# A hybrid attention / SSD backbone in fp32: layer 1's short convolution in token order, and a wider margin for the SSD groups

## The chip, the core and the metric

One NeuronCore of one Trainium2 chip runs the whole program in one launch. The metric is the device time of that launch in microseconds (us). The five engines have their own instruction queues: PE (TensorE, matmuls and transposes), DVE (VectorE), ACT (ScalarE), POOL (GpSimd) and SP (SyncE, which here issues most DMAs). In this program each engine works through its instructions in the order in which they were written, so one that waits holds all that stand behind it on the same engine.

## The reference, cut to what matters

Two layers over 256 latent tokens of width 2048, with 256 context tokens beside the first. Layer 0 (even) joins 16 heads of neighbourhood attention with a bidirectional Mamba-2 SSD of 8 groups; layer 1 (odd) is a gated short convolution. Every layer is normed, modulated by a conditioning vector, and added to the stream through a gate. The part that the change rewrites is layer 1:

```python
def short_conv_mixer(h, w_in, conv_w, w_out):
    p = h @ w_in                                   # 2048 -> 4 * 2048
    bg, cg, hv, g = jnp.split(p, 4, axis=-1)
    y = bg * dw_conv(cg * hv, conv_w)              # 3 taps along the tokens, one set per channel
    return (jax.nn.silu(g) * y) @ w_out
```

The other half of the change touches the order in which layer 0's SSD groups are placed. In a group the decay matrix exp(cs_i - cs_j) between tokens is built for four heads, multiplied with C B^T, and applied to x by matmuls.

## The kernel before

**Arithmetic.** All big projections are fp32 by three fp32r matmuls: activations and weights are each split in a high and a low part (`hH`/`hL`, `WH`/`WL`), and high x high, high x low and low x high are summed in PSUM. A weight block of 128 x 1024 values (512 KB) is loaded by SP into one of five `raw` buffers (`issue`, L367), cast by ACT into one of three places `w` (`split`, L403; the cast has line 422), and its low part is made by DVE (`low_part`, L426; line 429). From the output projection on, three more places are cut out of buffers that are free by then (KL, QT with QL, and wH with wL): six in all. `mm` is line 196, `turn` (a transpose by the identity) line 200.

**Order.** The program has no loop on the chip: Python writes out every instruction once, in an order that a planner decides. `Plan` (L38) keeps a modelled time for each engine and for each buffer. The main line of the program writes the matmuls of the projections, chunk by chunk, and after each few of them calls `pump` (L279), which looks at the tasks in three lists, `urgent`, `side` and `back`. A task is a generator that yields what it needs next: an engine, the buffers that must be ready, and a number of PSUM banks (`W_`). `may` (L247) lets it go on if the plan says that this engine would not have to wait. For PE the line is

```python
return rdy + (0 if isurg else 800) <= now + 100
```

that is, work of a `side` task on PE is let out only when its operands have been ready, by the plan, for 0.7 us. Where the main line cannot go on (no free bank, a row not made yet), `force` (L300) takes the task that can start earliest, without asking `may`. Tasks also hold shares of two budgets: 9 buffers `tmp` of 128x512 and 8 `half` of 128x256. `take` gives the buffer that was used longest ago.

**SSD groups.** `group_gen(s, gi)` (L1503) runs for each of 8 groups as a `side` task with 4 `tmp` and 4 `half` (spawned in `do_ssd`, L1640). Its steps: C B^T on PE; two reads for each half of the group of decay rows from DRAM scratch `csr` by SP (L1524); ACT and DVE steps (L1533 to L1553) that end in the product `Ds` of decay and C B^T (L1553, DVE); 16 matmuls `bank<-tmp,xtm` on PE, for which the task waits by `W_("PE", Ds[3], nb=1)`, and after which its `tmp` are given back; then gate, squares, a matmul that sums them (`sqs[0]`), a power on POOL (L1595), a transpose of the factor (`r2`), DVE (L1605), and `put_mix` (L1003, with lines 1008 and 1010), which splits the rows for the output projection. The output projection of layer 0 takes the pairs of mix rows in the order 0 to 5, 8 to 15, 6, 7 (L565); the last SSD group's pair is number 15, so 14th in that order. Its first pass makes two column groups of 512 at once.

**Layer 1.** For each of four column blocks i (512 channels) the parts cg, hv, g, bg are projected in this order, each with 8 weight blocks of 12 matmuls (96), into two PSUM banks (token tiles t = 0, 1; 128 tokens on the partitions). Each part is followed by an `urgent` task, and `ordered` (L1992) lets these tasks run one after the other:

- `cg_gen` (L2012): ACT copies cg out of PSUM.
- `hv_gen` (L2020): DVE makes u = hv x cg (L2025). Then `over` (L2003) turns u, four 128x128 transposes for each pair of channel tiles, so that channels lie on the partitions. Now a tap is a scalar of a partition: ACT multiplies the middle tap (L2032), DVE adds the two shifted taps (L2036, L2038) out of PSUM into v. All taps carry a factor 0.5 (`scwh`, L988).
- `gg_gen` (L2042): sg = (tanh(g/2) + 1) g, in token order (L2045, L2047).
- `bg_gen` (L2050): sg times bg (L2053); `over` turns the product; DVE multiplies it with v (L2058); ACT and DVE split the result into high and low (L2064, L2066) as `y2`, the stationary operand of the last projection.

Then four parts of 96 matmuls with `sc_out` follow, each ended by `fin_gen` (L2094).

Of the kernel before, what the change touches and what calls it, by code (L numbers as in the profile page):

```python
# [8 lines left out]
F32 = mybir.dt.float32  # L9
F32R = mybir.dt.float32r  # L10
AF = mybir.ActivationFunctionType
ALU = mybir.AluOpType
# [25 lines left out]
class Plan:  # L38
# [5 lines left out]
    def __init__(self):  # L44
        self.t = dict.fromkeys(("PE", "DVE", "ACT", "POOL", "SP"), 0.0)
        self.w, self.r, self.last = defaultdict(float), defaultdict(float), defaultdict(float)
        self.dma = 0.0
        self.pool = (0.0, 0.0)
# [85 lines left out]


class Task:
    def __init__(self, gen, tmps=0, halves=0):
        self.gen, self.tmps, self.halves, self.cond, self.on = gen, tmps, halves, None, False


@with_exitstack
def kernel(ctx: ExitStack, tc, x, cx, ada0, w0, adaT, w_in, w_out, sc_in, sc_out, rpb, small, const,
                       strict, rows, out):
    nc = tc.nc
    PS = bass.MemoryType.PSUM
    sb = ctx.enter_context(tc.tile_pool(name="sb", bufs=1))
# [3 lines left out]
    V, S, G, T, DMA = nc.vector, nc.scalar, nc.gpsimd, nc.tensor, nc.sync  # L150
    DMA2 = nc.scalar
    plan = Plan()
    E = plan.add

    def st(shape, tag, dt=F32, name=None):
        return sb.tile(list(shape), dt, tag=tag, name=name or tag, bufs=1)
# [29 lines left out]
    def take(pool):  # L186
        b = min(pool, key=lambda a: plan.last[a.tensor.name])
        pool[:] = [a for a in pool if a is not b]
        return b

    tmp, half, raw_ = (lambda: take(free_t)), (lambda: take(free_h)), (lambda: take(free_r))
# [6 lines left out]
    def turn(o, i):  # L198
        k = i.shape[0]
        E(T.transpose(o, i, ident if k == 128 else ident[:k, :k]))  # L200


    urgent, side, back = [], [], []
# [2 lines left out]
    budget = [NTMP, NHALF]  # L206
    reserve = [0]

    def spawn(q, gen, tmps=0, halves=0):
        q.append(Task(gen, tmps, halves))  # L210

    def cap(task, tmps, halves):
        budget[0] += task.tmps - tmps
# [26 lines left out]
    def grow(task):  # L240
        _, t, h = task.cond
        if t - task.tmps > budget[0] or h - task.halves > budget[1]:
            return False
        cap(task, t, h)
        return True

    def may(task, hor, isurg):  # L247
        eng, aps, nb = task.cond
        if eng == "if":
            return aps()  # L250
        if eng == "grow":
            return grow(task)
        if nb and len(free_b) < nb + (0 if isurg else reserve[0]):
            return False
        if eng == "DVE":
            lows_try()
        now, t = plan.t["PE"], plan.t["ACT" if eng == "AQ" else eng]
        rdy = plan.ready(aps)
        if eng == "AQ":
            return t <= now + hor and rdy <= t  # L260
        if hor < 2000 and nb and sorted(plan.last[b.tensor.name] for b in free_b)[nb - 1] + 3000 > now:
            return False
        if hor < 2000:
            rdy += 4000 if eng == "PE" else 2000 if eng == "DVE" else 0
        if eng == "PE":
            if nb:
                rdy = max(rdy, sorted(plan.last[b.tensor.name] for b in free_b)[nb - 1])
            return rdy + (0 if isurg else 800) <= now + 100
        if eng == "SP":
            return rdy <= max(t, now) + 200  # L270
        return t <= now + hor and rdy <= max(t, now) + 400
# [79 lines left out]
    P_ = lambda n: sm[:, _off[n][0]:_off[n][1]]  # L351
# [311 lines left out]
    hH, hL = [None] * KB, [None] * KB  # L663
# [320 lines left out]
    E(V.tensor_scalar(out=cwh, in0=P_("cw"), scalar1=0.5, scalar2=None, op0=ALU.mult))  # L984
    cbh = st([128, 32], "cbh")
    E(V.tensor_scalar(out=cbh, in0=P_("cb"), scalar1=0.5, scalar2=None, op0=ALU.mult))
    scwh = st([128, 48], "scwh")
    E(V.tensor_scalar(out=scwh, in0=P_("scw"), scalar1=0.5, scalar2=None, op0=ALU.mult))  # L988
    gqk = st([128, 1], "gqk")
    E(V.scalar_tensor_tensor(out=gqk, in0=P_("qg"), scalar=float(128 ** -0.5), in1=P_("kg"), op0=ALU.mult, op1=ALU.mult))  # L990

# [386 lines left out]
    Btm = [None]  # L1378
# [245 lines left out]
    def do_ssd(s, nxt):  # L1624
        if s:
            psB = banks(2)
            proj(256, 512, psB, 1)
            spawn(urgent, make_b(s, psB), 3)
        psC, = banks(1)
        proj(256, 256, [psC], 4)  # L1630
        spawn(urgent, make_c(s, psC), 0, 2)
        psX = banks(4)
        proj(512, 512, psX, 2)
        for gi in range(2):
            spawn(urgent, make_x(s, gi, psX[2 * gi:2 * gi + 2]), 3)
        psZ = banks(2)
        proj(512, 256, psZ, nxt)
        spawn(urgent, silu2_gen("Z", s, psZ, sz, lambda: ssd_done[0] >= 2 * s and ("K", 0) in got), 1)
        for gi in range(2):
            spawn(side, group_gen(s, gi), 4, 4)  # L1640

    spawn(urgent, make_b(0, psB0), 3)
    do_g(0, 1)
# [3 lines left out]
    for k in range(2):  # L1647
        W, _ = use()
# [4 lines left out]
        used()  # L1653
    spawn(urgent, dt_gen(psD), 1, 3)
    do_ssd(0, 2)

    def do_qk(a, nxt):
# [99 lines left out]
    late = [None] * 8 + \  # L1757
# [162 lines left out]
    for ns in ((0, 512), (1024,), (1536,)):  # L1920
        pss = [banks(2) for n in ns]
        for ip in range(16):
# [8 lines left out]
            if hold[0]:  # L1931
# [49 lines left out]


    y2 = [None] * KB
    scw = scwh.rearrange("p (k c) -> p k c", k=3)
    flat = lambda ap: ap.rearrange("p b c -> p (b c)")
    v = st([128, 4, 256], "Btm", name="v")
    cg, u = [], []
    sg = [st([128, 512], f"V{k}", name=f"sg{k}") for k in "HL"]

# [30 lines left out]
    def hv_gen(i, ps):  # L2020
        for t in range(2):
            yield W_("DVE", ps[t])
            if i == 0:
                u.append(tmp())
            E(V.tensor_tensor(out=u[t], in0=ps[t], in1=cg[t], op=ALU.mult))  # L2025
            give(free_b, ps[t])
        for b in range(0, 4, 2):
            pt = yield from over(u, b)
            yield W_("ACT", pt)
            for k in range(2):  # L2030
                ch = 4 * i + b + k
                E(S.mul(v[:, b + k, :], pt[:, k * 256:k * 256 + 256], scw[:, 1, ch:ch + 1]))  # L2032
            for k in range(2):
                ch, o = 4 * i + b + k, k * 256
                yield W_("DVE", v[:, b + k, :])
                E(V.scalar_tensor_tensor(out=v[:, b + k, 1:256], in0=pt[:, o:o + 255], scalar=scw[:, 0, ch:ch + 1],  # L2036
                                         in1=v[:, b + k, 1:256], op0=ALU.mult, op1=ALU.add))
                E(V.scalar_tensor_tensor(out=v[:, b + k, 0:255], in0=pt[:, o + 1:o + 256], scalar=scw[:, 2, ch:ch + 1],  # L2038
                                         in1=v[:, b + k, 0:255], op0=ALU.mult, op1=ALU.add))
            give(free_b, pt)  # L2040

    def gg_gen(i, ps):  # L2042
        for t in range(2):
# [6 lines left out]
    def bg_gen(i, ps):  # L2050
        for t in range(2):
            yield W_("DVE", ps[t])
            E(V.tensor_tensor(out=sg[t], in0=ps[t], in1=sg[t], op=ALU.mult))  # L2053
            give(free_b, ps[t])
        for b in range(0, 4, 2):
            pt = yield from over(sg, b)
            yield W_("DVE", pt)
            E(V.tensor_tensor(out=flat(v[:, b:b + 2, :]), in0=pt, in1=flat(v[:, b:b + 2, :]), op=ALU.mult))  # L2058
            give(free_b, pt)
            yield W_("ACT", v[:, b:b + 2, :])  # L2060
            for k in range(2):
                kb = 4 * i + b + k
                hl = st([128, 2, 256], f"hH{kb}", F32R, name=f"y2_{kb}")
                E(S.copy(hl[:, 0], v[:, b + k, :]))  # L2064
                yield W_("DVE", hl[:, 0])
                E(V.tensor_tensor(out=hl[:, 1], in0=v[:, b + k, :], in1=hl[:, 0].bitcast(F32), op=ALU.subtract))  # L2066
                y2[kb] = hl

    for i in range(4):
        for part, gen in ((1, cg_gen), (2, hv_gen), (3, gg_gen), (0, bg_gen)):  # L2070
            ps = banks(2)
# [60 lines left out]
    force(lambda: not urgent, (urgent,))  # L2132


_INS = ['x', 'cx', 'ada0', 'w0', 'adaT', 'w_in', 'w_out', 'sc_in', 'sc_out', 'rpb', 'small', 'const', 'strict', 'rows']


# [68 lines left out]
```

## Time and profile before

| | us |
|---|---|
| median of 3 runs | 1748.62 |
| lowest and highest run | 1746.23, 1752.42 |
| the profiled execution | 1747.58 |
| its span, first to last instruction | 1745.5 |
| PE busy | 1722.7 |
| DVE busy | 1240.2 |
| ACT busy | 783.5 |

Mean granted clock of TensorE: 0.999. HBM is read at 217 GB/s over the span.

How to read the rows below. Rows of groups are: line, engine, operation, out<-in by the program's buffer names (numbers left out), shapes, xcount | busy us, mean ns of one | idle time of the engine just before them and what ended most of it. A row of the chain of work that ended last is: start us, us, what. A row of the timeline is: start us, us, engine, line, operation, xcount, and in brackets the idle time before it with its releaser. A row of windows has the stretch, its length, then the busy time (and count) of PE, PEld, DVE, ACT and POOL, the granted clock of TensorE, the busy share of the DMA engines, and GB/s; restricted to one tile, it counts only the instructions that touch it. PEld is the load of the stationary operand. Rows of DMA issues are: out<-in, queue, xcount, KB each, median us from issue to landing. Records of matmuls overlap, so the length of a record is not the distance between two.

### The profile page before, as it was taken

The page shows a single profiled execution, that of the slowest core. Times are in us where ns is not written, and L with a number is a line of the kernel's source. Part 1 is how long each engine was busy: PE and PEld are TensorE (multiplying, and loading weights), DVE is VectorE, ACT ScalarE, POOL GpSimd, SP SyncE. Part 2 cuts the span into 40 slices and gives each one's busy share as a digit, 9 for nine tenths or more (in the row PEclk, how much of TensorE's full clock was granted, in tenths as well). Part 3 has the DMA queues.
Part 4 walks back from the last instruction along what each step waited for, and adds up shares of the span by engine and source line. Part 5 has one row for each costly group of instructions (what it writes and reads, how often), then busy time and mean ns, then how long its engine had stood idle before and what let it go on. Part 6 is the DMA issues. An engine that isn't in the chain of part 4 may idle for free.

```text
span 1745.5 us, 24824 instructions
## 1 busy us (share of the span) xinstructions
PE 1722.7 (99%) x9269; PEld 1453.6 (83%) x9269; DVE 1240.2 (71%) x2098; ACT 783.5 (45%) x1383; POOL 33.8 (2%) x28
## 2 busy tenths in 40 slices
PE   6999999999999999999999999999999999999998
PEld 4777989889888889888888898888888888888887
DVE  5697878868476878476868597887668666665554
ACT  5434544446244445244435243664445444444442
POOL 0000100001000001000001000000000000000000
PEclk9999999999999999999999999999999999999999
DMA  9997644666654676654766567767757777776563
GB/s 369 367 322 269 204 135 150 197 207 193 220 161 142 215 206 212 204 172 144 224 201 198 162 197 233 239 209 272 281 195 254 258 249 261 241 254 192 193 211 114
DMA packets 193671, 381.05 MB, mean 218 GB/s; under 512 B 18128, under 2 KB 57872, under 8 KB 193296
## 3 DMA queue, kind: packets, MB, share of 16 engines
q1 hardware_dynamic: 186272, 372.90, 66.2%
q10 hardware_dynamic: 7280, 6.59, 1.1%
q8 instruction: 72, 1.18, 0.3%
q14 instruction: 47, 0.39, 0.1%
HBM read 371.93 MB, written 7.50 MB: 217 GB/s over the span
## 4 chain that ended last, share of the span: by engine, by line
PE 94%; DMA 2%; DVE 2%; ACT 0%; issue 0%; SPq 0%; POOL 0%; DVEq 0%; ACTq 0%
PE bank L196 91%; PE bank L200 3%; DMA tmp<-dram_csr 1%; DMA raw<-in_ada 1%; DMA PT<-in_ada 1%; DVE w L429 0%; DVE csb L859 0%; DVE raw L859 0%; DVE raw L885 0%; ACT w L422 0%; ACT tmp L1533 0%; SPq L603 0%; DVE gt L818 0%; DVE tmp L1548 0%; DVE sz L818 0%
## 5 line engine op out<-in xcount | busy, mean ns | idle before, releaser
L429 DVE TENSOR_TENSOR w<-raw,w 128x1024 fp32r<-128x1024 f32 (+1 forms) x344 | 417.5, 1216 | 266.4 <-ACT w L422 264.8
L422 ACT CAST w<-raw 128x1024 fp32r<-128x1024 f32 (+1 forms) x344 | 360.0, 1048 | 545.3 <-PE bank L196 449.8
L196 PE MATMUL bank<-hH,w 128*128 128x256 f32 (+1 forms) x2064 | 485.4, 324 | 0.0
L196 PE MATMUL bank<-w,hH 128*128 128x512 f32 x1280 | 405.4, 395 | 3.4 <-ACT hH L780 2.5
L196 PEld LDWEIGHTS bank<-hH,w 128*128 128x128 f32 x2064 | 345.0, 188 | 32.2 <-issue 1.4
L196 PE MATMUL bank<-hL,w 128*128 128x256 f32 (+1 forms) x1040 | 334.8, 322 | 0.0
L196 PEld LDWEIGHTS bank<-w,hH 128*128 128x128 f32 x1280 | 236.9, 188 | 55.8 <-issue 3.2
L196 PE MATMUL bank<-w,hL 128*128 128x512 f32 x640 | 249.6, 390 | 0.1
L196 PEld LDWEIGHTS bank<-hL,w 128*128 128x128 f32 x1040 | 196.6, 189 | 14.8
L196 PE MATMUL bank<-w,h 128*128 128x512 f32 x768 | 179.6, 390 | 0.0
L196 PEld LDWEIGHTS bank<-w,h 128*128 128x128 f32 x768 | 143.6, 188 | 29.6
L885 DVE CUSTOM_DVE_ANT_0 raw<-raw,csb 128x1024 f32<-128x1024 f32 x128 | 155.4, 1218 | 4.4 <-DMA raw<-in_adaT 4.1
L196 PEld LDWEIGHTS bank<-w,hL 128*128 128x128 f32 x640 | 120.1, 188 | 25.7 <-DVE hL L792 0.9
L196 PE MATMUL bank<-w,mix 128*128 128x512 f32 x588 | 139.1, 392 | 0.0
L196 PEld LDWEIGHTS bank<-w,mix 128*128 128x128 f32 x588 | 109.2, 188 | 22.0 <-DVE w L429 0.3
L1368 DVE SCALAR_TENSOR_TENSOR tmp<-bank,cwh,tmp 128x508 f32<-128x508 f32 (+1 forms) x96 | 71.2, 745 | 1.9
L196 PE MATMUL bank<-KL,h 128*128 128x512 f32 x264 | 63.7, 389 | 0.0
L429 DVE TENSOR_TENSOR QL<-raw,QT 128x1024 fp32r<-128x1024 f32 x32 | 39.2, 1224 | 29.1 <-ACT QT L422 29.1
L429 DVE TENSOR_TENSOR wL<-raw,wH 128x1024 fp32r<-128x1024 f32 x31 | 37.9, 1224 | 30.0 <-ACT wH L422 30.0
L196 PEld LDWEIGHTS bank<-KL,h 128*128 128x128 f32 x264 | 49.5, 188 | 10.3
L429 DVE TENSOR_TENSOR KL<-raw,KL 128x1024 fp32r<-128x1024 f32 x32 | 39.2, 1224 | 26.5 <-ACT KL L422 26.5
L196 PE MATMUL bank<-QT,h 128*128 128x512 f32 x168 | 56.3, 392 | 0.0
(305 smaller groups left out, 1976.9 us busy)
## 6 DMA issues: line engine op xcount, KB each, us to landing
raw<-in_w_in SPq DMA_DIRECT2D x196, 512.0 KB, 3.8
raw<-in_adaT SPq DMA_DIRECT2D x128, 512.0 KB, 4.7
raw<-in_sc_in SPq DMA_DIRECT2D x128, 512.0 KB, 4.3
raw<-in_w_out SPq DMA_DIRECT2D x64, 512.0 KB, 5.0
raw<-in_ada SPq DMA_DIRECT2D x35, 512.0 KB, 8.0
raw<-in_sc_out SPq DMA_DIRECT2D x32, 512.0 KB, 3.7
raw<-in_w SPq DMA_DIRECT2D x16, 512.0 KB, 5.6
tmp<-dram_csr SPq DMA_DIRECT2D x32, 256.0 KB, 6.5
```

The source lines that it names most:

```text
L196: E(T.matmul(o, l, r, start=start, stop=stop, skip_group_check=True))
L200: E(T.transpose(o, i, ident if k == 128 else ident[:k, :k]))
L422: E(S.copy(H, v))
L429: E(V.tensor_tensor(out=Lo, in0=v, in1=H.bitcast(F32), op=ALU.subtract))
L885: E(V.tensor_tensor_reduce(out=raw, in0=raw, in1=csb, scale=1.0, scalar=0.0, op0=ALU.mult, op1=ALU.add, accum_out=gp[:, h, m:m + 1]))
L1368: E(V.scalar_tensor_tensor(out=do, in0=di, scalar=cwh[:, 32 * k + ch:32 * k + ch + 1], in1=do, op0=ALU.mult, op1=ALU.add))
```

## The change

Layer 1's u is no longer turned. `hv_gen` writes u in token order to a DRAM scratch of 258 rows, one for each column block (rows 1 to 256; rows 0 and 257 are set to zero once), reads back for each token tile the rows shifted by one token down and up into the `cg` buffers, and reads the three taps of its 512 channels, each spread over all partitions, from a new input `scr`. DVE then multiplies and adds buffers of 128x512 with each other. `bg_gen` multiplies sg by 0.5 and bg, then by v, in token order; `over` turns this product, and `y2` is split straight out of PSUM. All transfers are issued on SP. `v` changes shape from [128, 4, 256] to [128, 2, 512] in the same place. `scwh` keeps its place and is not computed.

Separately, a task may carry a number `late`, which is added to the 800 in `may` for PE work; the SSD groups get 3000.

```diff
-            return rdy + (0 if isurg else 800) <= now + 100
+            return rdy + (0 if isurg else 800 + task.late) <= now + 100
...
-            spawn(side, group_gen(s, gi), 4, 4)
+            spawn(side, group_gen(s, gi), 4, 4, 3000)
...
-    v = st([128, 4, 256], "Btm", name="v")
+    v = st([128, 2, 512], "Btm", name="v")
+    ud = [drt([258, 512], f"u{i}") for i in range(4)]
...
             E(V.tensor_tensor(out=u[t], in0=ps[t], in1=cg[t], op=ALU.mult))
             give(free_b, ps[t])
-        for b in range(0, 4, 2):
-            pt = yield from over(u, b)
-            yield W_("ACT", pt)
-            for k in range(2):
-                ch = 4 * i + b + k
-                E(S.mul(v[:, b + k, :], pt[:, k * 256:k * 256 + 256], scw[:, 1, ch:ch + 1]))
+        yield ("grow", 5 if i == 0 else 3, 0)
+        wr = [tmp() for _ in range(3)]
+        if i == 0:
+            E(V.memset(wr[0][:2], 0.0))
+            yield W_("SP", wr[0])
+            for d in ud:
+                z = d[0:1, :]
+                E(DMA.dma_start(bass.AP(tensor=z.tensor, offset=z.offset, ap=[[257 * 512, 2], [1, 512]]), wr[0][:2]))
+        yield W_("SP", *u, *wr)
+        for t in range(2):
+            E(DMA.dma_start(ud[i][1 + 128 * t:129 + 128 * t, :], u[t]))
+        for k in range(3):
+            E(DMA.dma_start(wr[k], scr[k, i * 512:(i + 1) * 512].partition_broadcast(128)))
+        for t in range(2):
+            yield W_("SP", *cg, ud[i])
             for k in range(2):
-                ch, o = 4 * i + b + k, k * 256
-                yield W_("DVE", v[:, b + k, :])
-                E(V.scalar_tensor_tensor(out=v[:, b + k, 1:256], in0=pt[:, o:o + 255], scalar=scw[:, 0, ch:ch + 1],
-                                         in1=v[:, b + k, 1:256], op0=ALU.mult, op1=ALU.add))
-                E(V.scalar_tensor_tensor(out=v[:, b + k, 0:255], in0=pt[:, o + 1:o + 256], scalar=scw[:, 2, ch:ch + 1],
-                                         in1=v[:, b + k, 0:255], op0=ALU.mult, op1=ALU.add))
-            give(free_b, pt)
+                E(DMA.dma_start(cg[k], ud[i][128 * t + 2 * k:128 * t + 2 * k + 128, :]))
+            yield W_("DVE", wr[1])
+            E(V.tensor_tensor(out=v[:, t], in0=u[t], in1=wr[1], op=ALU.mult))
+            for k in range(2):
+                yield W_("DVE", cg[k], wr[2 * k])
+                E(V.tensor_tensor(out=cg[k], in0=cg[k], in1=wr[2 * k], op=ALU.mult))
+                E(V.tensor_tensor(out=v[:, t], in0=v[:, t], in1=cg[k], op=ALU.add))
+        give(free_t, *wr)
...
-            E(V.tensor_tensor(out=sg[t], in0=ps[t], in1=sg[t], op=ALU.mult))
+            E(V.scalar_tensor_tensor(out=sg[t], in0=sg[t], scalar=0.5, in1=ps[t], op0=ALU.mult, op1=ALU.mult))
             give(free_b, ps[t])
+            E(V.tensor_tensor(out=sg[t], in0=sg[t], in1=v[:, t], op=ALU.mult))
         for b in range(0, 4, 2):
             pt = yield from over(sg, b)
-            yield W_("DVE", pt)
-            E(V.tensor_tensor(out=flat(v[:, b:b + 2, :]), in0=pt, in1=flat(v[:, b:b + 2, :]), op=ALU.mult))
+            for k in range(2):
+                kb, p_ = 4 * i + b + k, pt[:, k * 256:k * 256 + 256]
+                yield W_("ACT", pt)
+                hl = st([128, 2, 256], f"hH{kb}", F32R, name=f"y2_{kb}")
+                E(S.copy(hl[:, 0], p_))
+                yield W_("DVE", hl[:, 0])
+                E(V.tensor_tensor(out=hl[:, 1], in0=p_, in1=hl[:, 0].bitcast(F32), op=ALU.subtract))
+                y2[kb] = hl
             give(free_b, pt)
...
```

More of the change, by code (lines that the diff above doesn't have):

```diff
@@ L136, with __init__ @@
 class Task:
-    def __init__(self, gen, tmps=0, halves=0):
-        self.gen, self.tmps, self.halves, self.cond, self.on = gen, tmps, halves, None, False
+    def __init__(self, gen, tmps=0, halves=0, late=0):
+        self.gen, self.tmps, self.halves, self.late, self.cond, self.on = gen, tmps, halves, late, None, False
 @with_exitstack
 def kernel(ctx: ExitStack, tc, x, cx, ada0, w0, adaT, w_in, w_out, sc_in, sc_out, rpb, small, const,
-                       strict, rows, out):
+                       strict, rows, scr, out):
     nc = tc.nc
@@ L207, with spawn @@
     reserve = [0]
-    def spawn(q, gen, tmps=0, halves=0):
-        q.append(Task(gen, tmps, halves))
+    def spawn(q, gen, tmps=0, halves=0, late=0):
+        q.append(Task(gen, tmps, halves, late))
     def cap(task, tmps, halves):
@@ L986 @@
     E(V.tensor_scalar(out=cbh, in0=P_("cb"), scalar1=0.5, scalar2=None, op0=ALU.mult))
-    scwh = st([128, 48], "scwh")
-    E(V.tensor_scalar(out=scwh, in0=P_("scw"), scalar1=0.5, scalar2=None, op0=ALU.mult))
+    st([128, 48], "scwh")
     gqk = st([128, 1], "gqk")
@@ L1983 @@
     y2 = [None] * KB
-    scw = scwh.rearrange("p (k c) -> p k c", k=3)
-    flat = lambda ap: ap.rearrange("p b c -> p (b c)")
-    v = st([128, 4, 256], "Btm", name="v")
+    v = st([128, 2, 512], "Btm", name="v")
+    ud = [drt([258, 512], f"u{i}") for i in range(4)]
     cg, u = [], []
@@ L2052, in bg_gen @@
             yield W_("DVE", ps[t])
-            E(V.tensor_tensor(out=sg[t], in0=ps[t], in1=sg[t], op=ALU.mult))
+            E(V.scalar_tensor_tensor(out=sg[t], in0=sg[t], scalar=0.5, in1=ps[t], op0=ALU.mult, op1=ALU.mult))
             give(free_b, ps[t])
+            E(V.tensor_tensor(out=sg[t], in0=sg[t], in1=v[:, t], op=ALU.mult))
         for b in range(0, 4, 2):
             pt = yield from over(sg, b)
-            yield W_("DVE", pt)
-            E(V.tensor_tensor(out=flat(v[:, b:b + 2, :]), in0=pt, in1=flat(v[:, b:b + 2, :]), op=ALU.mult))
-            give(free_b, pt)
-            yield W_("ACT", v[:, b:b + 2, :])
-            for k in range(2):
[L2062 to L2067, printed above, removed]
+            for k in range(2):
[6 more added lines that the diff above has]
+                y2[kb] = hl
+            give(free_b, pt)
     for i in range(4):
@@ L2132 @@
     force(lambda: not urgent, (urgent,))
-_INS = ['x', 'cx', 'ada0', 'w0', 'adaT', 'w_in', 'w_out', 'sc_in', 'sc_out', 'rpb', 'small', 'const', 'strict', 'rows']
+_INS = ['x', 'cx', 'ada0', 'w0', 'adaT', 'w_in', 'w_out', 'sc_in', 'sc_out', 'rpb', 'small', 'const', 'strict', 'rows', 'scr']
 def kernel(**inputs):
@@ L2193 @@
         'small': small, 'const': const, 'strict': strict,
-        'rows': np.concatenate([f('ssd_dt_bias')[0].reshape(1, 64), f('ssd_a_log')[0].reshape(1, 64)], axis=1)}
+        'rows': np.concatenate([f('ssd_dt_bias')[0].reshape(1, 64), f('ssd_a_log')[0].reshape(1, 64)], axis=1),
+        'scr': f('sc_conv_w')[0]}
     nc = bacc.Bacc("TRN2", target_bir_lowering=False, num_devices=1, dynamic_dma_scratch_size=1024)
```

## The prediction, made before the changed kernel ran

> **What bounds the kernel now.** I read the page first: its span, the busy shares, and the chain of work that ended last.
>
> ```profile
> span 1745.5 us, 24824 instructions
> ...
> PE 1722.7 (99%) x9269; PEld 1453.6 (83%) x9269; DVE 1240.2 (71%) x2098; ACT 783.5 (45%) x1383; POOL 33.8 (2%) x28
> ...
> PE 94%; DMA 2%; DVE 2%; ACT 0%; issue 0%; SPq 0%; POOL 0%; DVEq 0%; ACTq 0%
> ```
>
> PE (TensorE) is idle for 22.8 of 1745.5 us and carries 94% of the chain. So an edit counts if it takes instructions off PE, or a gap out of PE; work put on DVE or DMA counts only where it makes PE wait. The next view is the list of waits, of PE alone, to see what gaps there are. The columns are the waiter, the releaser, total us, times, longest.
>
> ```profile
> PE bank L196 <- DMA raw<-in_ada: 10.8, 1, 10.8
> ...
> PE bank L196 <- DVE tmp L1553: 1.9, 1, 1.9
> ```
>
> The 10.8 us are the first load and stay. The 1.9 us are the only wait of PE after 160 us: a matmul of `group_gen`, released by its line 1553. That is the place of the change's second half. The chain in order of time and the timeline show how it came about.
>
> ```profile
> 893.20 10.12 DMA tmp<-dram_csr
> ...
> 910.88 6.42 DMA tmp<-dram_csr
> ```
>
> ```profile
> 918.97 0.87 PE L196 MATMUL bank<-tmp,xtm 128*64 128x128 f32 x10
> ...
> 921.22 0.42 DVE L1553 TENSOR_TENSOR tmp<-tmp 128x256 f32<-128x256 f32 x1
> ...
> 921.70 0.65 PE L196 MATMUL bank<-tmp,xtm 128*64 128x128 f32 x6 [1.86 <-DVE tmp L1553]
> ```
>
> Two reads of decay rows took 10.1 and 6.4 us, the second ended late, and PE had been given the 16 matmuls of the group too early: it did 10, then stood 1.86 us until line 1553 had made the third operand. After the gap the windows of 2 us show the clock.
>
> ```profile
> 920.00:922.00 2.00, 0.30 (x5) 0.31 (x6) 1.97 (x7) 2.00 (x7) 0.00 (x0) 1.00 0.98 308
> 922.00:924.00 2.00, 2.00 (x12) 1.47 (x8) 1.97 (x5) 2.00 (x14) 0.00 (x0) 0.76 0.69 270
> 924.00:926.00 2.00, 2.00 (x6) 1.63 (x5) 1.97 (x4) 2.00 (x18) 0.00 (x0) 0.50 0.39 84
> 926.00:928.00 2.00, 2.00 (x9) 1.62 (x9) 1.97 (x5) 1.85 (x8) 0.00 (x0) 0.89 0.97 268
> 928.00:930.00 2.00, 2.00 (x11) 1.65 (x10) 0.25 (x3) 1.26 (x5) 1.67 (x1) 1.00 0.73 228
> ```
>
> The third figure from the end is the granted clock: 1.00 in the gap, then 0.76, 0.50 and 0.89, then 1.00 again. Lost beside the gap: 2 x (0.24 + 0.50 + 0.11) = 1.70 us.
>
> **Part 1, the transposes of u.** In layer 1 each of four column blocks turns u (8 transposes, line 200) and later the gated sg (8). The change drops the first set: 32 transposes.
>
> ```profile
> L200 PE MATMUL bank<-const,tmp x32: 270/273/273, 1342.8 to 1610.3; 128*128 128x128 f32 x32
> ```
>
> ```profile
> 1342.96 0.87 PE bank L200 x8
> 1343.83 43.55 PE bank L196 x192
> ...
> 1431.83 0.87 PE bank L200 x8
> ...
> 1658.43 82.32 PE bank L196 x363
> ```
>
> A record lasts 273 ns, but they overlap: in the chain eight take 0.87 us. Matmuls beside them keep their pitch (82.32 / 363 = 0.2268, 43.55 / 192 = 0.2268), so nothing more hangs on the switch. 4 x 0.87 = **3.5 us** come off PE. In these windows PE has no idle time that could swallow it.
>
> [...]
>
> **Part 2, the convolution in token order.** What it costs the other engines, by rows of layer 1:
>
> ```profile
> L2038 DVE SCALAR_TENSOR_TENSOR v<-bank,scwh,v 128x255 f32<-128x255 f32 x16 | 7.7, 483 | 0.6
> L2036 DVE SCALAR_TENSOR_TENSOR v<-bank,scwh,v 128x255 f32<-128x255 f32 x16 | 7.6, 475 | 1.1 <-ACT v L2032 1.1
> ...
> L2032 ACT ACTIVATE v<-bank,scwh 128x256 f32<-128x256 f32 x16 | 6.3, 474 | 5.1 <-PE bank L200 5.1
> ...
> L2058 DVE TENSOR_TENSOR v<-bank,v 128x512 f32<-128x512 f32 x8 | 5.5, 684 | 0.0
> ...
> L1742 DVE TENSOR_TENSOR x1a<-tmp,tmp 128x512 f32<-128x512 f32 x2 | 1.4, 692 | 0.1
> ```
>
> ```profile
> 1341.00:1385.00 44.00, 44.00 (x200) 36.52 (x199) 31.55 (x39) 19.21 (x22) 0.00 (x0) 1.00 0.74 242
> 1385.00:1430.00 45.00, 45.00 (x204) 37.28 (x203) 29.61 (x35) 19.06 (x22) 0.00 (x0) 1.00 0.82 260
> ```
>
> DVE loses 4 x (0.483 + 0.475) = 3.8 us a block and gains ten products and sums of 128x512 between buffers at 0.69 = 6.9. In `bg_gen` two products (0.684) are replaced by two of 0.69, and y's low halves read the bank instead of v: with 0.684 from a bank against 0.692 from buffers, nothing. That is +3.1 us a block, against 89 - 61.2 = 27.8 us that DVE stands idle in the 89 us of the first block. ACT loses 4 x 0.474. Cost on PE: nothing, while that slack lasts. The half factor that moves into `bg_gen`, and the scaling of scw that goes, cost nothing that can be seen.
>
> DMA: a block adds nine transfers of 256 KB on SP's queue (two writes of u, three weight rows, four shifted reads), 2.4 MB in 89 us, so 26 GB/s on some 250; the share of 0.74 to 0.82 rises by about a tenth. The first block adds four small zero writes. Their time to landing is not in the trace; the nearest rows:
>
> ```profile
> tmp<-dram_csr SPq DMA_DIRECT2D x32, 256.0 KB, 6.5
> ...
> tmp<-dram_mrow SPq DMA_DIRECT2D x12, 256.0 KB, 5.3
> ...
> out<-tmp SPq DMA_DIRECT2D x8, 256.0 KB, 4.0
> ...
> dram_csr<-tmp ACTq DMA_DIRECT2D x1, 64.0 KB, 2.0
> ```
>
> A write lies between 2.0 and 4.0 us; I take 4.0, since size and queue are the same. A read lies between 5.3 and 10.1 (the worst csr read above); I take 5.3, whose rows are whole and contiguous as here. The chain after hv's sums: products 1.4, write 4.0, read 5.3, five DVE steps 3.5, second read 5.3, five steps 3.5 = 23.0 us (33 with the worst reads). It has to be there when bg's product needs v:
>
> ```profile
> 1340.95 1.37 DVE L2025 TENSOR_TENSOR tmp<-bank,tmp 128x512 f32<-128x512 f32 x2 [2.45 <-PE bank L196]
> ...
> 1365.25 0.58 ACT L2045 ACTIVATE sgH<-bank 128x512 f32<-128x512 f32 x1
> ...
> 1385.56 0.68 DVE L2053 TENSOR_TENSOR sgH<-bank,sgH 128x512 f32<-128x512 f32 x1
> ```
>
> 1340.95 + 23.0 = 1364, and the product comes at 1385.56: 21.6 us to spare, 12 at the worst. (`gg_gen` is held until `hv_gen` ends; at 1365.25 it would hardly notice.)
>
> The added waits: SP waits for u's write before the shifted reads, with the weight loads behind it; DVE waits for the reads, with low halves (line 429) behind it. Both work ahead:
>
> ```profile
> L429 DVE TENSOR_TENSOR w<-raw,w 128x1024 fp32r<-128x1024 f32 (+1 forms) x344 | 417.5, 1216 | 266.4 <-ACT w L422 264.8
> L422 ACT CAST w<-raw 128x1024 fp32r<-128x1024 f32 (+1 forms) x344 | 360.0, 1048 | 545.3 <-PE bank L196 449.8
> ...
> raw<-in_sc_in SPq DMA_DIRECT2D x128, 512.0 KB, 4.3
> ```
>
> The last columns of the first two rows are idle time and what ended it: the split on ACT waits for PE to release a place, not the reverse. There are six places, and one weight block is 12 matmuls (2.72 us); less the one in use, the split (1.05) and the low half (1.22), that leaves 5 x 2.72 - 2.3 = 11.3 us before a held DVE holds PE. A held SP has the five raw buffers ahead of that as well (5 x 2.72 - 4.3 - 2.3 = 7.0 us more). Waits of a few us cost nothing. Range of part 2 on PE: 0 to the case below.
>
> **Part 3, `late=3000`.** The planner lets out a group's PE work only when it is 3.8 us overdue by plan, not 0.8. The 16 matmuls would start at about 918.97 + 3 = 922.0, after the 921.65 at which the missing operand was there. So the gap goes: 1.86, and with it the clock's 1.70 = **3.6 us**; bounds 0 (the gap stays) and 3.6. Nothing is left to take: it was the only one.
>
> [...]
>
> The price is later groups. Three PE steps of each group are delayed by up to 3 us: its products, its sums of squares, its turned factor. The last group is the tight one. It begins when the one before frees its buffers (3 us later), so up to 12 us are added.
>
> ```profile
> 1175.11 0.76 DVE L1010 TENSOR_TENSOR mix<-half,mix 128x256 fp32r<-128x256 f32 x2
> ```
>
> ```profile
> 1105.00:1190.45 85.45, 75.02 (x312) 1.00 0.69 228
> ```
>
> Its pair of mixes was ready at 1175.9. The output projection takes 24 matmuls for each pair of mixes in its first pass and needs this pair as its 14th, so after 13 x 24 = 312, at 1190.45. 14.6 us of room against 12: it holds, with 2.6 left.
>
> **The sum** against the profiled execution (1747.58; span 1745.5, 2.1 around it): 3.5 + 3.6 = 7.1, so 1740.5. That execution lies 1.0 below the median of 1748.62; on the median the forecast is **1741.6 us**.
>
> **Rivals.** *The gap stays or comes back elsewhere.* The margin holds only where the planner is free; `force`, which finds banks, ignores it, and every later matmul of layer 0 shifts by some us in an order that so far left one gap. For it: csr reads scatter from 6.4 to 10.1 us. Against it: PE had no other wait in 1500 us. Then only the transposes count: 1748.6 - 3.5 = 1745.1.
>
> [...]
>
> *The projection waits for the last group.* If the delays add to 18 us and not 12, PE stands 18 - 14.6 = 3.4 us, and with 1.7 for the clock that returns 5.1: 1746.6; with as much again for the group before it, 1751.7.
>
> *DVE is held behind the shifted reads: slower.* Twice a block DVE stands in front of a read, and the low halves stand behind it. If it falls 11.3 us behind, PE waits, four times. At 16 us a block each time costs 4.7 + 1.7 for the clock: 4 x 6.4 - 7.1 = +18.5, so 1767. Slower by 0.3% (5.2 us) takes (5.2 + 7.1) / 4 = 3.1 a block, so a lag of 11.3 + 3.1 - 1.7 = 12.7 us. One csr read reached 10.1; two late reads in a row would do. Against it: 27.8 us of idle DVE a block, and the 5.3 us that such reads mostly take.
>
> **Chances.** Forecast 0.58; gap 0.17; clock 0.04; projection 0.11; DVE held 0.10. 0.3% (5.2 us) is about what a measurement can tell from no change, and the forecast lies only 1.8 beyond it. Faster: 0.50 of the forecast, 0.02 of gap, 0.02 of clock = 0.54. Same: 0.08 + 0.15 + 0.02 + 0.07 = 0.32. Slower: 0.04 + 0.10 = 0.14. The range reaches from 1737 (the scatter of runs below the forecast, 1746.23 against 1748.62, and as much again) over gap and the milder projection to 1749; outside lie DVE held and the worse projection.
>
> **What would show it.** Line 200 in layer 1 with 32 transposes, not 64, and the distance between two blocks' first turns down from 88.9 us by 0.9. No wait of PE on line 1553, granted clock 1.00 from 160 us on. DVE waits on shifted reads of some us, without a PE wait behind them. The last mix split before its 312th matmul. Wrong would be: any PE wait on a weight's low half in layer 1 (DVE held), on a mix (projection), or another group line (gap).

## The result, and the profile after

The changed kernel takes 1744.74 us (median of 19 runs, 1741.2 to 1748.02) against 1747.97 us for the kernel before (19 runs, 1743.46 to 1752.42). The ratio is 0.9977, 95% interval 0.9969 to 0.9986. That is 4.0 us faster, with 2.4 to 5.4 us as the interval. (Here and below, a difference in us is worked out from the ratio and the median of before; the two medians themselves lie 3.2 us apart.) The ratios go by the fast runs alone: one run of e2 (3528.13 us) and one of e3 (1911.59 us) are counted in the tables below and left out of the ratios. The forecast was a gain of 7.1 us. The profiled execution took 1743.12 us.

The page of the changed kernel, span, busy shares, and the chain by engine:

```profile
span 1741.3 us, 24796 instructions
...
PE 1718.7 (99%) x9237; PEld 1450.3 (83%) x9237; DVE 1251.3 (72%) x2106; ACT 776.8 (45%) x1367; POOL 33.9 (2%) x28
...
PE 94%; DMA 3%; DVE 2%; ACT 0%; issue 0%; SPq 0%; POOL 0%; DVEq 0%; ACTq 0%
```

PE has 32 instructions fewer and is busy 4.0 us less. DVE is busy 11.1 us more (the forecast: 4 x 3.1 = 12.4), ACT 6.7 less (4 x 4 x 0.474 = 7.6). PE still carries the chain. The chain in order of time through layer 1 shows the transposes that stay:

```profile
1390.69 0.87 PE bank L200 x8
1391.56 85.71 PE bank L196 x378
1477.28 0.87 PE bank L200 x8
1478.15 87.07 PE bank L196 x384
1565.22 0.87 PE bank L200 x8
```

One set of eight a block is left. From one block to the next it is 1565.22 - 1477.28 = 87.94 us, where two blocks' first turns stood 88.87 apart before: 0.93 us less a block, 3.7 for four. (The first distance, 86.59, is shorter because 378 matmuls lie in it and not 384.)

The list of what PE waits for, in the changed kernel:

```profile
PE bank L196 <- ACT hH L780: 2.5, 2, 1.4
PE bank L196 <- DVE w L429: 1.7, 2, 1.3
```

(Each number after the colon: total us, times, longest.) The row on the decay product (line 1553 before, 1552 now) is gone, and a row that was not there has come: 1.7 us on a weight's low half (line 429), in two places: 0.43 where the output projection begins, at 1112.86, and this one in layer 0, close behind the first SSD groups, in the timeline:

```profile
405.21 0.50 PE L196 MATMUL bank<-hH,w 128*128 128x256 f32 x2 [1.32 <-DVE w L429]
```

A window near the start shows one more loss that the profile of before did not have (the figure before the last two is the granted clock):

```profile
24.20:27.65 3.45, 3.45 (x9) 2.70 (x9) 3.35 (x5) 2.81 (x5) 0.00 (x0) 0.51 1.03 412
```

3.45 us at 0.51 cost 1.7. So between these two executions, whose spans differ by 4.2 us: 3.7 from the transposes and 3.56 from the old gap and its clock came off; 1.32, 0.43 and 1.7 came back. That makes 3.8; the other 0.4 lies in small gaps and in the scatter of the records. The question for the experiments is which of these belong to the kernel and which to the one execution.

### The profile page after: what moved, and what is told of

It is laid out like the page before. It is cut to its first block, busy times and chain, and to the rows that moved or that the text cites. A ratio compares the mean times of both kernels' runs of the same rounds, so it can differ in the third digit from the quotient of the medians.

```text
span 1741.3 us, 24796 instructions
## 1 busy us (share of the span) xinstructions
PE 1718.7 (99%) x9237; PEld 1450.3 (83%) x9237; DVE 1251.3 (72%) x2106; ACT 776.8 (45%) x1367; POOL 33.9 (2%) x28
## 4 chain that ended last, share of the span: by engine, by line
PE 94%; DMA 3%; DVE 2%; ACT 0%; issue 0%; SPq 0%; POOL 0%; DVEq 0%; ACTq 0%
PE bank L196 91%; PE bank L200 3%; DMA raw<-in_ada 1%; DMA tmp<-dram_mixd 1%; DMA csb<-dram_crow 1%; DVE w L429 0%; DMA bias<-in_rpb 0%; DVE csb L859 0%; DVE raw L885 0%; DVE mix L1704 0%; DVE tmp L1547 0%; SPq L603 0%; SPq L383 0%; DVE raw L859 0%; DVE bias L1146 0%
## 5 line engine op out<-in xcount | busy, mean ns | idle before, releaser
L196 PE MATMUL bank<-wH,h 128*128 128x512 f32 x168 | 55.3, 389 | 0.0
L429 DVE TENSOR_TENSOR wL<-raw,wH 128x1024 fp32r<-128x1024 f32 x31 | 37.9, 1222 | 20.6 <-ACT wH L422 20.6
```

Of the source, the lines that this page charges most:

```text
L196: E(T.matmul(o, l, r, start=start, stop=stop, skip_group_check=True))
L429: E(V.tensor_tensor(out=Lo, in0=v, in1=H.bitcast(F32), op=ALU.subtract))
```

## The experiments

**Theory**: the transposes give their 3 to 4 us in every execution; the margin's 3.6 us were a gap that one execution happened to have, and the margin pays for what it removes with new waits elsewhere. **Rival 1**: the margin works as forecast, and the convolution eats a part of it by holding SP or DVE. **Rival 2**: the transposes are worth less than their chain time.

### The two halves apart, and the price of a transpose

The first takes the changed kernel without its margin; the second takes the margin alone into the kernel before; the fourth makes each transpose of u four times, into the same bank, in the kernel before (96 more).

```diff
 e1_conv_alone (from the changed kernel)
-            spawn(side, group_gen(s, gi), 4, 4, 3000)
+            spawn(side, group_gen(s, gi), 4, 4)
 e2_margin_alone (from the kernel before)
...
-            return rdy + (0 if isurg else 800) <= now + 100
+            return rdy + (0 if isurg else 800 + task.late) <= now + 100
...
-            spawn(side, group_gen(s, gi), 4, 4)
+            spawn(side, group_gen(s, gi), 4, 4, 3000)
 e4_turns_fourfold (from the kernel before)
-    def over(rows_, b):
+    def over(rows_, b, times=1):
...
+        for _ in range(times):
...
-            pt = yield from over(u, b)
+            pt = yield from over(u, b, 4)
```

> The change without its margin: the SSD groups are placed as before, so layer 0 is written in the order of before, and only layer 1 differs. Theory A (the 32 transposes are worth their pitch, 3.5 us, and the margin nothing on the average of runs): 3.5 us faster than before, no different from the whole change. Theory B (the margin pays 3.6 us, and the convolution gives its 3.5 us back to waits behind DVE or the reads): within 1 us of before. If the gap before line 1553 is a matter of this order and not of one execution, its profile shows it again, 1 to 3 us long.

> The kernel before with 3000 added to the margin of the SSD groups and nothing else. Theory A: within 1 us of before; its profile has no wait on line 1553, but one of 1 to 2 us on a weight's low half near 400 us, as in the profile of the whole change. Theory B: 3.6 us faster than before, with no such wait.

> The kernel before with each transpose of u in layer 1 made four times into the same bank: 96 transposes more, nothing else changed. At the pitch of the chain (0.109 us) that costs 10.5 us; at the length of a record (0.272) 26 us; if the transposes lay beside other work, nothing. It gives the price of the 32 transposes that the change drops, with three times the signal.

Measured against 22 runs of the kernel before (median 1748.46):

| kernel | median us (runs) | ratio (95%) | us |
|---|---|---|---|
| e1_conv_alone | 1743.75 (10) | 0.9973 (0.9961 to 0.9985) | -4.7 (-6.8 to -2.6) |
| e2_margin_alone | 1748.08 (12) | 0.9998 (0.9987 to 1.0008) | -0.3 (-2.3 to +1.4) |
| e4_turns_fourfold | 1757.66 (6) | 1.0055 (1.0036 to 1.0074) | +9.6 (+6.3 to +12.9) |

96 transposes cost 9.6 us, 0.100 us each, so the 32 that the change drops are worth 3.2 (2.1 to 4.3). In the chain of e4 a set of 32 takes 3.49 us, 0.109 each:

```profile
1342.62 3.49 PE bank L200 x32
```

Rival 2 falls, and so does the 0.273 us that the record's length would give. The convolution alone brings all that the whole change brings, and the margin alone brings nothing that 12 runs can see. Rival 1 falls with it: there is no gain of the margin for the convolution to eat.

### Was the gap that the margin was to close there every time?

Two more executions show it: the kernel before unchanged (e10_before_again, one run), and the changed kernel unchanged (e5_whole_again).

> The kernel before, once more with a profile. If the gap of 1.9 us at 920 us belongs to this order, it is there again; if it was one execution's (the two kernels whose layer 0 has the same order did not show it there), it is not, and gaps stand elsewhere or nowhere.

> The whole change once more, on the chip and beside the runs of before that the next three share. Both theories: 3 to 4 us faster than before, as on the first chip. Its profile should show the wait on a weight's low half near 404 us again if that wait belongs to the order, and not if it was one execution's.

e10 took 1747.59 us, the same as the first profile's 1747.58. The same order of the same instructions stands at the same matmul as before, in its timeline, for a third of the time, and in its list of waits there are two such places, not one:

```profile
922.92 0.65 PE L196 MATMUL bank<-tmp,xtm 128*64 128x128 f32 x6 [0.57 <-DVE tmp L1553]
```

```profile
PE bank L196 <- DVE tmp L1553: 1.2, 2, 0.7
```

The gap of 1.86 was 0.57, with the clock at 1.00 behind it (921 to 929 us); another of 0.67 stood at 391. Two more profiles have the same layer 0: in e4 neither is there, and in e1 the one at 922 is missing while the one near 391 lasts 1.69. So the place at 922 stood 1.86, 0.57, 0 and 0 us in four profiles of one order. The place is weak in this order, but how long PE stands there differs between executions; one profile's 1.86 + 1.70 was the largest of four draws.

e5 gave 1745.03 (11 runs), ratio 0.9974 (0.9966 to 0.9983): the change's gain once more. In its list of waits the new row on line 429 stands again, with 2.3 us in three places: two near 400 us, and 0.41 us where the output projection begins.

### Where the margin pays, and where it costs

The margin holds for the groups of all four quarters. e3 keeps it for the third quarter only (the one whose group had the gap), e6 for the first only, both with the convolution; e11 takes the third quarter's margin alone into the kernel before; e9 turns the margin round.

```diff
 e3_margin_s2 (from the changed kernel)
-            spawn(side, group_gen(s, gi), 4, 4, 3000)
+            spawn(side, group_gen(s, gi), 4, 4, 3000 if s == 2 else 0)
 e6_margin_s0 (from the changed kernel)
-            spawn(side, group_gen(s, gi), 4, 4, 3000)
+            spawn(side, group_gen(s, gi), 4, 4, 3000 if s == 0 else 0)
 e9_margin_negative (from the changed kernel)
-            spawn(side, group_gen(s, gi), 4, 4, 3000)
+            spawn(side, group_gen(s, gi), 4, 4, -2500)
 e11_margin_s2_alone (from e2_margin_alone)
-            spawn(side, group_gen(s, gi), 4, 4, 3000)
+            spawn(side, group_gen(s, gi), 4, 4, 3000 if s == 2 else 0)
```

> The whole change, but with the margin for the two groups of the third SSD quarter alone (those of the gap at 920 us): what stands before 880 us keeps the order of before. Theory A, with the new wait near 400 us as its cause: that wait goes and the gap at 920 us stays away, so 1 to 3.5 us faster than the whole change (4.5 to 7 faster than before). Theory B: as the whole change. If the order after 880 us brings other gaps, no gain over the whole change.

> The whole change, but with the margin for the first two SSD groups alone. Theory A, refined: the margin does harm at the first groups (waits on low halves between 400 and 407 us, 1.3 to 2.7 us) and good at the third quarter's. So waits near 400 us in its profile, and 2.5 to 3.5 us faster than before, 1 to 3 us slower than the kernel with the margin at the third quarter alone (which was 7.0 us faster than before). Rival (the margin is worth the same anywhere, the differences are scatter): no wait near 400 us, 4 to 7 us faster than before.

> The whole change with a margin of 2500 less in place of 3000 more: PE gets the groups' matmuls 1.7 us before the plan has their operands. It is to make gaps of many lengths on PE. [...] The time is 10 to 40 us above the whole change.

> The kernel before with the margin for the two groups of the third SSD quarter and nothing else. If the halves add up: 1.5 to 3 us faster than before (the three kernels with it and the convolution were 6.5 to 7.0 us faster, the convolution alone 4.7). If the difference between them was scatter: within 1 us of before.

| kernel | median us (runs) | ratio (95%) | us |
|---|---|---|---|
| e3_margin_s2 | 1742.56 (7) | 0.9960 (0.9946 to 0.9974) | -7.0 (-9.4 to -4.5) |
| e6_margin_s0 | 1746.17 (8) | 0.9976 (0.9965 to 0.9987) | -4.2 (-6.1 to -2.3) |
| e11_margin_s2_alone | 1746.59 (12) | 0.9991 (0.9979 to 1.0004) | -1.6 (-3.7 to +0.7) |
| e9_margin_negative | 1782.64 (1) | not taken | some +34 beside the kernel before, +38 beside the changed one |

First the cost. PE's new wait near 400 us is in all four profiles with the margin in the first quarter (1.32 in the changed kernel; 0.55, 0.76 and 1.16 in e5; 0.61, 0.76 and 1.51 in e2; 1.03 in e6) and in none of the eight that have an order with margin 0 there (before, e1, e3, e4, e7, e8, e10, e11). It belongs to the margin. (A low half makes PE wait 1.0 us in e4 and e8 too, but at 234 us, ahead of the first groups.) How it comes about, in the changed kernel's chain:

```profile
394.02 7.55 DMA bias<-in_rpb
401.58 0.02 issue
401.60 1.21 DVE bias L1146 x6
402.81 0.07 DVE r L1592
402.88 1.13 DVE raw L885
404.01 0.01 DVE gp L885
404.02 1.15 DVE w L429
```

and in its timeline, then in that of e3 with no margin there:

```profile
394.02 4.86 SPq L1141 DMA_DIRECT2D bias<-in_rpb  x6
...
401.60 1.21 DVE L1146 TENSOR_TENSOR bias<-bias,const 128x128 f32<-128x128 f32 x6 [1.04 <-DMA bias<-in_rpb]
```

```profile
396.33 2.80 SPq L1141 DMA_DIRECT2D bias<-in_rpb  x6
...
401.27 1.16 DVE L1146 TENSOR_TENSOR bias<-bias,const 128x128 f32<-128x128 f32 x6
```

With the margin the group's own steps slide past other work, and the attention's bias loads come 2.06 us behind the two csr reads on SP (391.96 to 394.02; 3.65 without it, 392.68 to 396.33). Their issue takes 4.86 us, not 2.80, DVE stands 1.04 us for them, and what is queued behind that wait on DVE is a reduction (line 885) and then the low half (line 429) that PE needs. It is just such a wait "with low halves behind it" as the prediction priced for layer 1, in layer 0, where the prediction did not look. The same chain leads to the wait in e2 and e6, with a bias load of 7.55 and 7.42 us for which DVE stands 1.23 and 0.76; in e5 DVE stands 0.88 for it. That the shift of the order brings the wait is shown by the twelve profiles; the steps between are read from the traces and were not tried one by one.

In the same stretch the margin also takes a wait away. Without it PE waits for the decay product near 391 us, for 1.80 us in e7, 1.69 in e1, 0.67 in e10, 0.49 in e11, 0.29 in e3 and not at all in before, e4 and e8; with it, never. So in the first quarter one wait that comes and goes is traded for another that was there in all four profiles.

Now the gain. e9 shows that the margin's direction is right: with 2.5 us taken off instead of 3 us added, PE's list has

```profile
PE bank L196 <- DVE tmp L1552: 12.0, 6, 4.2
...
PE bank L200 <- POOL r L1594: 8.5, 8, 1.1
PE bank L196 <- DVE half L1581: 4.1, 5, 1.7
```

and the kernel is 37.9 us above the changed kernel's median. But above 0 the curve is nearly flat. Against e1, the third quarter's margin brings 2.3 us in e3 (0.9973 to 0.9960); the intervals overlap, and e11, the same margin in the order before, shows 1.6 with zero inside its interval. What speaks for it is that e7 and e8 below, which carry it too, repeat e3's value. The first quarter's margin (e6) brings nothing beside e1. So, as an estimate: the margin gains about 2 us in the third quarter, nothing or a little less than nothing in the first, and about nothing if given to all.

e3 is thus the fastest kernel here: by its ratio 7.0 us faster than the one before, by the medians 5.9. Beside the whole change (0.9977, and 0.9974 in e5) the three with the same margin have 0.9960, 0.9962 and 0.9963, about 2.5 us; the intervals overlap.

### How near the convolution came to costing something

The prediction's slower rival was a convolution that holds DVE until PE waits. No profile shows a PE wait in layer 1. Two kernels test how far it is: e7 moves all the convolution's transfers to POOL's queue, off SP; e8 adds a second trip of u through DRAM (read back unshifted, written again) in two of four blocks. Both have e3's margin.

```diff
 e7_pool_queue (from e3)
-        yield W_("SP", *u, *wr)
+        yield W_("POOL", *u, *wr)
...
-                E(DMA.dma_start(cg[k], ud[i][128 * t + 2 * k:128 * t + 2 * k + 128, :]))
+                E(G.dma_start(cg[k], ud[i][128 * t + 2 * k:128 * t + 2 * k + 128, :]))
 e8_second_round_trip (from e3)
+        if i in (0, 2):
+            yield W_("SP", *cg, ud[i])
+            for t in range(2):
+                E(DMA.dma_start(cg[t], ud[i][1 + 128 * t:129 + 128 * t, :]))
+            yield W_("SP", *cg)
+            for t in range(2):
+                E(DMA.dma_start(ud[i][1 + 128 * t:129 + 128 * t, :], cg[t]))
```

> The kernel with the margin at the third quarter alone, and all transfers of layer 1's convolution issued on POOL's queue, behind which nothing else stands, and not on SP's, behind which the weight loads stand. Theory: SP held behind u's write made the loads late and took the low halves' lead over PE from 11 us to 2.4 us at the first block, without a wait of PE in the profiles. So here the lead stays above 6 us in all blocks (as before the change), and the time is within 2 us of the kernel on SP's queue (5 to 8 us faster than before); a gain beyond that would mean that PE did wait there in other executions. Rival (the reads' traffic, not the held queue, took the lead): the lead falls to 2 to 4 us as well.

> The kernel with the margin at the third quarter alone, and in the first and third column block of layer 1 u is written, read back unshifted and written again before the shifted reads, so that SP is held twice more. If a held SP is what takes the lead: the low halves come late by 5 to 10 us more, PE waits 2 to 7 us on a low half at the first block (lead 2.7 us) and little or not at the third (lead 8.8 us), and the time is 2 to 9 us above the kernel without it. If the lead does not hang on SP, no wait of PE in layer 1 and no difference beyond 2 us.

Against 20 runs of the kernel before (median 1749.69) e7 took 1743.72 (6 runs), 0.9962 (0.9949 to 0.9975), and e8 1743.28 (5 runs), 0.9963 (0.9950 to 0.9975): both the same as e3. That e7 changes no time says that SP's holding costs nothing, not that there is none. The holding can be seen. SP and the engines behind it in the first block, timeline of the changed kernel, and the same stretch before:

```profile
1343.81 1.22 SPq L2032 DMA_DIRECT2D dram_u<-tmp  x4
1345.07 0.83 SPq L2035 DMA_DIRECT2D dram_u<-tmp  x2
1347.47 1.29 SPq L2037 DMA_DIRECT2D tmp<-in_scr  x3
1348.80 4.23 SPq L385 DMA_DIRECT2D raw<-in_sc_in  x4
...
1357.98 1.05 ACT L422 CAST w<-raw 128x1024 fp32r<-128x1024 f32 x1 [10.40 <-DMA raw<-in_sc_in]
...
1359.06 1.22 DVE L429 TENSOR_TENSOR w<-raw,w 128x1024 fp32r<-128x1024 f32 x1 [2.94 <-ACT w L422]
...
1361.74 1.75 PE L196 MATMUL bank<-w,h 128*128 128x512 f32 x7
```

```profile
1344.63 8.77 SPq L385 DMA_DIRECT2D raw<-in_sc_in  x5
```

The weight loads go out at 1348.80 where they went out at 1344.63: four zero writes, two writes of u, a wait of 1.4 us before the weight rows may overwrite the buffer that the zeros come from, and three rows of weights stand ahead of them. Four loads then go out close together, and the first lands 9.2 us after its issue, where the same load before took 4.6. The cast stands 10.4 us for it, the low half ends at 1360.28, and PE's twelve matmuls on it begin with the fifth in the last row, 1361.74 + 4 x 0.227 = 1362.65. The low half leads PE by 2.4 us there.

Worked out in the same way for each weight block from the fifth of layer 1 on, the median lead is 11.1 us before and 10.4 in the changed kernel (the forecast's slack: 11.3). The weight block above led by 11.1 us before, so 8.7 of its lead went. The other profiles with this layer 1 show the same: 2.1 to 3.0 in e1, e3, e5, e6 and e9. On POOL's queue (e7) the same block leads by 10.3, so it was the held queue that took the lead, and not the transfers' traffic. Once the weights land, the casts start 1.35 us apart (1357.98, 1359.32, 1360.68), where PE takes 2.72 for a block, and the lead grows to 5.1 us; but it falls once more, to 3.1 at 1398.9, and is back above 8 only at 1412.

That e8 would make PE wait was wrong, but e8 is not the test that it was meant to be. In its order the weight loads go out ahead of the second trip, as its timeline of SP shows:

```profile
1347.23 3.24 SPq L385 DMA_DIRECT2D raw<-in_sc_in  x4
1350.56 1.41 SPq L2039 DMA_DIRECT2D tmp<-dram_u  x2
```

The same weight block leads by 8.7 us there, more than without the second trip. The least lead behind the convolution's start in e8, 2.8 us, stands at 1419, in the second column block, which has no second trip; its cause is open. So how much longer SP could be held before PE waits is not shown.

The transfers themselves took longer than forecast, but not always. Rows of DMA issues, median us from issue to landing, of the changed kernel and of e7:

```profile
tmp<-dram_u SPq DMA_DIRECT2D x16, 256.0 KB, 9.2
...
dram_u<-tmp SPq DMA_DIRECT2D x8, 256.0 KB, 4.7
```

```profile
tmp<-dram_u POOLq DMA_DIRECT2D x16, 256.0 KB, 7.0
```

In e3, with the same layer 1, the reads took 5.3. v was nevertheless there: the last of block 0's additions ends at 1374.6, and the product that needs v starts at 1384.65, in the changed kernel's timeline:

```profile
1373.94 0.69 DVE L2047 TENSOR_TENSOR v<-v,tmp 128x512 f32<-128x512 f32 x1
...
1384.65 0.69 DVE L2063 TENSOR_TENSOR sgH<-sgH,v 128x512 f32<-128x512 f32 x1
```

10.0 us to spare, close to the 12 of the prediction's worst reads.

## Why the prediction was right or wrong

**What bounds the kernel**: right. PE carries 94% of the chain in both, and only what leaves PE or opens a gap in it moved the time: 11.1 us more of DVE and nine more transfers a block cost nothing that the runs can see.

**Part 1, 3.5 us**: right. 3.7 by the blocks' distance, 3.2 (2.1 to 4.3) by the price of e4, and e1's 4.7 (2.6 to 6.8) holds both.

**Part 2, nothing**: right in its result, and the cover was the one named, the lead of the weight split. Two sizes were off. The cover of a held SP, 11.3 + 7.0 us, took 4.3 us for a load; held back and sent four together, the first load took 9.2, and 2.4 us of lead were left where the weight block had 11.1. And of the two added waits it was SP's that came near to PE, not DVE's, on which the rival was built: DVE stood 5.45 us for the weight rows in the first block, but the low half behind it came late for its cast, and the cast had stood 10.4 us for weights that SP had sent late.

**Part 3, 3.6 us: the step that failed.** (By the line in `may` the margins are 0.7 and 3.7 us, not the 0.8 and 3.8 of the working; nothing hangs on that.) It read: "So the gap goes: 1.86, and with it the clock's 1.70 = 3.6 us", and "Nothing is left to take: it was the only one". The gap goes, yes: in the changed kernel's profiles line 1552 holds PE nowhere. But its worth was taken from one execution, and it is 0.57, 0 and 0 us in three others of the same order. And the bounds, "0 (the gap stays) and 3.6", left out a loss: the same 3 us of delay shift the order around the first groups, where they open 1.0 to 2.9 us of waits on PE that no order without them has there. Net of both the margin alone gained 0.3 us, with an interval from 2.3 gained to 1.4 lost. The rival "the gap stays or comes back elsewhere" named the effect (a gain of 3.5; measured 4.0), with the right reason: matmuls of layer 0 shift in an order that so far left one gap. It had 0.17 where the forecast had 0.58. That the change came out faster, as forecast, is the work of part 1 alone, as far as the runs can tell.

**The clock's dip**: it came behind other gaps of about this size in e7 (1.80 us, then 3.40 us at a mean of 0.51) and e6 (2.19 us, at 149 us, then 3.60 us at a mean of 0.53), but not behind 1.69 us in e1 (1.00 up to 397.60 us). So the 1.70 us that part 3 added for it were likely, not certain. The chance of 0.04 for the clock was for a dip that stays when the gap goes: in the changed kernel, without the gap, the clock is 1.00 from 900 to 940 us.

**The projection waits for the last group**: no. The row of the last pair of mixes, in the changed kernel's timeline:

```profile
1180.30 0.42 DVE L1009 TENSOR_TENSOR mix<-half,mix 128x256 fp32r<-128x256 f32 x1
```

It ends at 1180.7, 4.8 us later than before, not 12, and its matmul comes at 1189.9: 9.2 us of room. The delays do not add up group by group as the working had it.

**The sum**: 7.1 forecast, 4.0 (2.4 to 5.4) measured. Take part 3 at the 0.3 that it gained and part 1 at 3.5, and it is 3.8. Half of the forecast gain was not there to be had; what saves the forecast's range is that it was drawn to take in the rival.

## What to carry to other kernels

A gap of one or two us in one profile can be a draw (the one at 922 us stood 1.86, 0.57, 0 and 0 us in four): look at the same place in a second execution of the same order before pricing it, and count the clock's share as likely rather than certain (of the gaps of 1.69, 1.80, 1.86 and 2.19 us above, the last three had about half the clock behind them). A change to an order's margin moves every later step, so price the waits it may open as well as the one it closes, and try it at the one place where it is wanted. When a cover is worked out from buffer counts, check it at the very place where the new wait goes in, and follow the queue that issues the cover's own loads.

## What the runs showed of the hardware

**The granted clock behind a gap of PE.** Six gaps, by the timelines, lists of waits and windows of six profiles:

| run | PE's gap, us | granted clock behind it |
|---|---|---|
| the kernel before | 1.86, up to 921.70 | 0.76, 0.50 and 0.89 in three windows of 2 us from 922 on |
| e6 | 2.19, near 149 | mean of 0.53 from 149.40 to 153.00 |
| e7 | 1.80, up to 392.81 | mean of 0.51 from 394.20 to 397.60 |
| e9 | 4.23, up to 392.61 | 0.50 from 392.60 to 395.90 |
| e1 | 1.69, up to 392.54 | 1.00 up to 397.60 |
| e10 | 0.57, up to 922.92 | 1.00 up to 929 |

The gaps of e7 and e1 are the same wait, for the decay product in the first quarter. Behind 1.80 us in e7 the clock halved for a while, behind 1.69 us in e1 it didn't:

```profile
392.80:394.20 1.40, 1.39 (x9) 1.08 (x10) 1.40 (x3) 0.93 (x4) 0.00 (x0) 0.96 0.39 149
394.20:397.60 3.40, 3.40 (x9) 2.63 (x8) 3.30 (x9) 0.95 (x3) 0.00 (x0) 0.51 0.59 166
397.60:399.00 1.40, 1.40 (x8) 1.15 (x7) 0.87 (x3) 0.00 (x0) 0.00 (x0) 1.00 0.79 227
```

```profile
392.70:394.20 1.50, 1.50 (x11) 1.15 (x10) 1.50 (x4) 1.00 (x3) 0.00 (x0) 1.00 0.35 135
394.20:397.60 3.40, 3.40 (x18) 2.85 (x17) 3.30 (x8) 0.90 (x3) 0.00 (x0) 1.00 0.66 192
```

The idle time does not tell such cases apart: in e9 PE was idle for 1.50 us between 395.90 and 399.30, less than in e1's gap, and the mean clock was 0.51 from 399.30 to 402.70. What decides it, these runs do not show.
